# A hybrid S5 and band attention step on one core: band corners written once into the bias table, queries and keys transposed four steps later, third token tile loaded sooner

## The chip, the core and the metric

The kernel runs on one core of one Trainium2 chip. The time is device time in microseconds (us) of one execution, given as the median of several runs. The engines are TensorE (PE; its weight loads are listed apart as PEld), VectorE (DVE), ScalarE (ACT), GpSimd (POOL) and SyncE (SP), which here issues nearly all the DMAs; POOL issues the rest. Each engine works through its instructions in program order, and so does a DMA queue with its issues.

## The reference, cut to what matters

One layer: RMS norm, one input projection into six groups of 512 columns, an S5 branch, band attention, and an output projection. 2048 prompt tokens (16 tiles of 128) and 8x16 tokens of running streams (tile 16).

```
h = _rms_norm(x, norm_gain)
z = jnp.einsum('bld,de->ble', h, w_in)
u, g_s, q, k, v, g_a = jnp.split(z, SPLITS, axis=-1)
y_s, hr, hi = _s5_branch(u, ...)
q = _rms_norm(heads(q), q_gain); k = _rms_norm(heads(k), k_gain)
y_a = _band_attention(q, k, v, rel_table)      # 8 heads x 64, own chunk of 64 and 8 before
mixed = concat([y_s * silu(g_s), y_a * silu(g_a)])
y = x + einsum('ble,ed->bld', mixed, w_out)
...
dist = arange(CHUNK)[:, None] + PAST_CHUNKS * CHUNK - arange(BAND * CHUNK)[None, :]
bias = rel_table[:, clip(dist, -128, 128) + 128]
s = where(valid, q @ k * HEAD_DIM ** -0.5 + bias, NEG_INF)
```

## The kernel before

**The foreground.** Every projection is made of steps, `mm3` (L189 to L191): three matmuls of 128x128 by 128x512, since each 32-bit operand is split into a high and a low part (high by high, low weight by high, high weight by low). `inproj` has three passes over the 17 token tiles in the order 16, 0, 1, ..., 15; pass 1 makes u and k, pass 2 v and q, pass 3 the two gates, 8 steps for each group: 816 steps. Then `glu` has 136 steps and `outproj` 272. A tile's activations come as `xraw` (L214), are split by ACT into `hhi` (L228) and two steps later by DVE into `hlo` (L231). Weights come in chunks of 128x512 (`load_w`, L139, 256 KB) into 5 raw buffers, and `conv_w` splits a chunk on ACT (`whi`, L155) and DVE (`wlo`, L156); the chunk that takes over the raw buffer is loaded right away at the start, and two steps later (`T_LW`) elsewhere. The last tile of a pass converts the 16 chunks of the next pass while it still works with its own.

**Queries and keys** (`ev_norm`). After the eighth step of a group ACT squares and scales the result (L274, L275). Two steps later `power` reduces on DVE (L279) and POOL takes the power (L280, L281); `T_SCALE` = 8 steps after the evacuation `scale` multiplies on DVE (`zs`, L284), and `T_TURN` = 14 steps after it `turn` puts four transposes on PE (L294), whose result ACT and DVE split (L303, L304) and SP stores into `kt_d` or `qt_d` (L244) two steps later and more. These delays are counted in steps by `defer` and `tick`.

**The background** is one generator, `bias_rows`, then `s5`, `decode` and `attention`, that is advanced between steps by a credit: 0.48 of a step's 650 in S5, nothing while weights are being converted, and in attention as many as the work that is left asks for, so that it ends 64 steps before the last. A `yield` of n costs n credits. What it emits stands in the engines' programs between the steps. In S5 of interest: `UT` transposes (P on ACT L719, PE L733, ACT L734) and `build_c` with the matmuls `pk` (L686), which follows the first `feed`.

**The bias.** `bias_rows` writes for each head a skewed table of 128 rows of 767 entries into `tl_d` (L965, one POOL DMA each). In attention each of 32 units loads a 128x640 tile from it (`bias`, L1114, on SP), and POOL sets two 64x64 corners of the tile, which lie outside the band, to a large number (L1115, L1116).

**The start.** `inproj` loads the first two tiles in quarters with 5 weight chunks between, converts chunks 0 to 15, and each conversion issues the load five chunks on; then `dma_h(2)` loads the third tile, and the first 32 steps run.

```
        for j in range(2):
            sumsq(TILES[j], tok[j])
            for _ in range(4):
                self.conv_w()
        dma_h(2)
```

Of the kernel before, what the change touches and what calls it, by code (L numbers as in the profile page):

```python
# [7 lines left out]
F32 = mybir.dt.float32  # L8
# [15 lines left out]
NH, HD = 8, 64  # L24
# [4 lines left out]
BIG = 1e30  # L29


def fv(ap):
    return ap.bitcast(F32)
# [6 lines left out]
def ap_of(t, offset, pat):  # L40
    return bass.AP(tensor=t.tensor, offset=t.offset + offset, ap=pat)


class Build:
# [97 lines left out]
    def conv_w(self):  # L142
        nc = self.nc
        n = self.nconv
        self.nconv += 1
        key, _, k = self.chunks[n]
        raw = self.raws.pop(n)
        hi = self.wp.tile([128, 512], F32R, tag="whi", name="whi", bufs=16)
        lo = self.wp.tile([128, 512], F32R, tag="wlo", name="wlo", bufs=16)
        if k is None:  # L150
            nc.scalar.activation(out=hi, in_=raw, func=AF.Copy)
            nc.vector.tensor_sub(lo, raw, fv(hi))
        else:
            gcol = self.gain[:, k:k + 1]
            nc.scalar.activation(out=hi, in_=raw, func=AF.Copy, scale=gcol)  # L155
            nc.vector.scalar_tensor_tensor(lo, raw, gcol, fv(hi), op0=OP.mult, op1=OP.subtract)  # L156
        self.W[key] = (hi, lo)
        if self.step:
            self.defer(self.T_LW, lambda: self.load_w(n + self.NR))
        else:  # L160
            self.load_w(n + self.NR)

    def due(self, start, gap, n):
        self.cq += [start + gap * j for j in range(n)]
# [28 lines left out]
    def inproj(self):  # L193
        nc, I, tc = self.nc, self.I, self.tc
# [9 lines left out]
        def load_tok(t):  # L204
            xt = xp.tile([128, 1024], F32, tag="xtok", name="xtok")
            nc.sync.dma_start(xt, x3[t])
            return xt

        def dma_h(i):
            if i >= len(seq):  # L210
                return
            ps, t = seq[i]
            raw = hp.tile([128, 8, 128], F32, tag="xraw", name="xraw", bufs=1)
            nc.sync.dma_start(raw, I["xT"][t])  # L214
            XR[i] = raw, load_tok(t) if ps == 0 else None
# [132 lines left out]
        n = 0  # L348
# [17 lines left out]
        for j in range(2):  # L366
            sumsq(TILES[j], tok[j])
            for _ in range(4):
                self.conv_w()
        dma_h(2)  # L370
        for k in range(8):
            for j in range(2):
                self.mm3(z0[j], H0[j][0][:, k], H0[j][1][:, k], W[0, 0, k], k == 0, k == 7)
# [75 lines left out]
    def s5(self):  # L449
        nc, I, tc = self.nc, self.I, self.tc  # L450
# [59 lines left out]
        c = 1.0 / (2.0 * math.pi)  # L510
# [171 lines left out]
        def build_c(b):  # L682

            pk = ps.tile([128, 128], F32, tag="ut", name="pk")
            for g in range(GB):
                nc.tensor.matmul(pk[32 * g:32 * g + 16], X[:, b * GB + g, :],  # L686
                                 CA[b][:, g, 0:8].rearrange("p j h -> p (j h)"), start=True, stop=True,
                                 tile_position=(0, 32 * g))
            KR[b] = pk

        def build_d(b):
            pk = KR[b]
            kr = KR[b] = mp.tile([16, GB, 128], F32, tag="bt", name="kr", bufs=1)
            for g in range(GB):
                nc.scalar.activation(out=kr[:, g], in_=pk[32 * g:32 * g + 16], func=AF.Copy)
            nc.vector.tensor_tensor(out=kr[:, :, 0:16], in0=kr[:, :, 0:16], in1=Deye[:, b * GB:(b + 1) * GB], op=OP.add)

        def build_e(b):
            kr = KR.pop(b)
            for j in range(8):  # L700
                nc.sync.dma_start(Tm[b % 2][16 * j:16 * j + 16, :, 16 * j:128], kr[:, :, 0:128 - 16 * j])  # L701
# [34 lines left out]
        def feed(n):  # L736

            def blk(m):
                return m // 3, m % 3
            if n + 3 < 3 * NBATCH:  # L740
                load_u(*blk(n + 3))
            if n + 1 < 3 * NBATCH:
                perm_u(*blk(n + 1))
            if n < 3 * NBATCH:
                step_a(*blk(n))
# [118 lines left out]
        SL = self.SL_S5  # L864
# [9 lines left out]
        for n in range(3):  # L874
            if n == 1:
                build_d(0)
            feed(n)
            if n == 0:
                build_c(0)
            if n == 2:  # L880
                build_e(0)
            yield SL
# [64 lines left out]
    def bias_line(self):  # L947
        nc, I = self.nc, self.I
        self.st_line = ExitStack()
        c = self.pool(self.st_line, "line", side="right")  # L950
        self.rl = c.tile([NH, 768], F32, name="rl")
        self.rr = c.tile([NH, 257], F32, name="rr")
        nc.gpsimd.dma_start(self.rr, I["rel"])

    def bias_rows(self):

        nc, rl, rr = self.nc, self.rl, self.rr
        nc.vector.tensor_scalar(self.qg2, self.qg2, -0.125, None, op0=OP.mult)
        nc.vector.tensor_scalar(rl[:, 511:768], rr, -1.0, None, op0=OP.mult)
        nc.vector.tensor_scalar(rl[:, 0:511], rr[:, 0:1].to_broadcast([NH, 511]), -1.0, None, op0=OP.mult)  # L960
        nc.gpsimd.dma_start(self.rl_d, rl)
        self.st_line.close()
        yield 600
        for h in range(NH):
            nc.gpsimd.dma_start(self.tl_d[h], ap_of(self.rl_d, 768 * h, [[0, 128], [1, 767]]))  # L965
            yield 1000


    def decode(self):
# [129 lines left out]
    def attention(self):  # L1099
        nc = self.nc  # L1100
        st = ExitStack()
        p = self.pool(st, "att", side="right", bufs=2)
# [8 lines left out]
        def bias(n):  # L1111
            if n < len(heads):
                b = p.tile([128, 640], F32, tag="bias", name="bias", bufs=3)
                nc.sync.dma_start(b, ap_of(self.tl_d, heads[n] * 128 * 767 + 127, [[766, 128], [1, 640]]))  # L1114
                nc.gpsimd.memset(b[64:128, 0:64], BIG)  # L1115
                nc.gpsimd.memset(b[0:64, 576:640], BIG)  # L1116
                BI[n] = b

        def load_k(n, old):
# [139 lines left out]
        SL = self.SL_ATT  # L1259
# [11 lines left out]
        for n in range(2):  # L1271
            bias(n)
            yield 3 * SL
# [4 lines left out]
        for i in range(N + 6):  # L1278
# [9 lines left out]
            if done:  # L1288
                n, s, a = subs[i - 2]
# [28 lines left out]
            if i < N:  # L1318
                n, r = x[0], i % 8
                if r == 2:  # L1320
                    load_ga(n)
                if n + 1 < len(units) and r < 6:
                    loads(n + 1)[r]()
                if r == 3:
                    bias(2 * n + 2)
                if r == 5:
                    bias(2 * n + 3)
# [153 lines left out]
    MARGIN = 0  # L1481
    att_left = 136
    C_PREP = 400
    T_SCALE, T_TURN = 8, 14
    WARM = 24
    A_START = 2
    W_PV, W_QT = 0.3, 1.2
# [119 lines left out]
```

## Time and profile before

| | |
|---|---|
| median of 3 runs | 1228.44 us (1226.21 to 1231.3) |
| the profiled execution | 1226.13 us |
| its span | 1224.3 us, 18936 instructions |
| mean granted TensorE clock | 0.995 of full speed |
| PE, PEld busy | 1193.0 us (97%), 983.1 us (80%) |
| DVE, ACT, POOL busy | 742.6 us (61%), 597.7 us (49%), 366.6 us (30%) |
| mm3 of the input passes (L189, L190, L191) | 339.2, 321.3 and 320.7 us, 816 each |
| DMA | 236.58 MB in 190119 packets, 58136 of them under 512 B |

The span is what the hardware profiler saw of one execution; the 1.8 us between it and the execution's time lie before and after. Busy times are the sums of one engine's instructions. In the timeline a matmul's row has its start and its modelled length, and overlaps the next one: the time that one takes is the distance from start to start, and the square bracket gives the idle time before it with what ended it.

### The profile page before, as it was taken

How to read it: one execution, taken by the hardware profiler on the slowest of the kernel's cores; microseconds unless marked ns; L12 is line 12 of the kernel's file. 1: busy time of each engine (PE TensorE's matmuls, PEld its weight loads, DVE VectorE, ACT ScalarE, POOL GpSimd, SP SyncE). 2: the span in 40 equal slices, each digit the busy share in tenths (PEclk: the TensorE clock that was granted, in tenths of full speed). 3: DMA queues.
4: the chain of work that ended last, by engine and by line, in shares of the span. 5: the costliest groups of instructions: out<-in, count | busy, mean ns of one | idle time of the engine just before them, and what ended most of it. 6: DMA issues, size and time to landing. Idle time of an engine off the chain costs nothing.

```text
span 1224.3 us, 18936 instructions
## 1 busy us (share of the span) xinstructions
PE 1193.0 (97%) x6687; PEld 983.1 (80%) x6687; DVE 742.6 (61%) x1391; ACT 597.7 (49%) x1159; POOL 366.6 (30%) x455
## 2 busy tenths in 40 slices
PE   8999999899999998999999999999999999999998
PEld 5788888777788876887777878788888888888876
DVE  5324556868999988985444456565565555555511
ACT  6434446266666656553232346565654555455410
POOL 2433242557767735540000011111211121121120
PEclk9999999999999998999999999999999999999999
DMA  8876556655545567433895688897877777767243
GB/s 252 262 250 181 155 177 202 195 142 129 149 123 151 135 195 214 110 93 88 270 382 171 204 247 245 255 265 205 217 221 215 206 240 241 196 205 225 73 136 107
DMA packets 190119, 236.58 MB, mean 193 GB/s; under 512 B 58136, under 2 KB 122656, under 8 KB 189000
## 3 DMA queue, kind: packets, MB, share of 16 engines
q1 hardware_dynamic: 189016, 232.15, 64.2%
q0 software_dynamic: 864, 3.21, 0.8%
q8 instruction: 53, 0.87, 0.3%
q14 instruction: 42, 0.34, 0.1%
q10 hardware_dynamic: 144, 0.00, 0.0%
HBM read 169.48 MB, written 67.80 MB: 194 GB/s over the span
## 4 chain that ended last, share of the span: by engine, by line
PE 78%; DMA 6%; DVE 6%; POOL 3%; ACT 3%; issue 2%; SPq 1%; DVEq 0%; ACTq 0%; POOLq 0%
PE z L189 19%; PE z L191 18%; PE z L190 18%; PE o L1218 6%; PE pt L1200 5%; PE s L1170 5%; DMA wraw<-in_w_in_dram 3%; PE pt L294 1%; PE o L1057 1%; PE y L843 1%; SPq L701 1%; PE y L842 1%; PE v L771 1%; ACT whi L155 1%; PE s L1015 1%
## 5 line engine op out<-in xcount | busy, mean ns | idle before, releaser
L189 PE MATMUL z<-whi,hhi 128*128 128x512 f32 x816 | 339.2, 416 | 1.4 <-ACT whi L155 0.7
L190 PE MATMUL z<-wlo,hhi 128*128 128x512 f32 x816 | 321.3, 394 | 3.3 <-DVE wlo L156 3.1
L191 PE MATMUL z<-whi,hlo 128*128 128x512 f32 x816 | 320.7, 393 | 0.5 <-DVE hlo L231 0.5
L189 PEld LDWEIGHTS z<-whi,hhi 128*128 128x128 f32 x816 | 154.1, 189 | 38.9 <-issue 5.1
L190 PEld LDWEIGHTS z<-wlo,hhi 128*128 128x128 f32 x816 | 154.5, 189 | 36.5 <-DVE wlo L156 8.0
L191 PEld LDWEIGHTS z<-whi,hlo 128*128 128x128 f32 x816 | 154.0, 189 | 34.3 <-DVE hlo L231 1.0
L1207 ACT ACTIVATE pth<-pt 128x640 fp32r<-128x640 f32 (+4 forms) x128 | 81.7, 639 | 129.3 <-PE pt L1200 89.4
L1208 DVE TENSOR_TENSOR ptl<-pt,pth 128x640 fp32r<-128x640 f32 (+4 forms) x128 | 94.6, 739 | 60.6 <-ACT pth L1207 59.7
L189 PE MATMUL z<-whi,mh 128*128 128x512 f32 x272 | 113.7, 418 | 0.0
L1115 POOL MEMSET bias<- 64x64 f32 x32 | 4.7, 146 | 363.5 <-DMA bias<-tl_d 250.0
L1189 ACT ACTIVATE sn<-sn,mn 128x640 f32<-128x640 f32 (+4 forms) x128 | 96.9, 757 | 29.5 <-DVE mn L1180 29.4
L191 PE MATMUL z<-whi,ml 128*128 128x512 f32 x272 | 107.1, 394 | 1.3 <-POOL ml L1415 1.3
L190 PE MATMUL z<-wlo,mh 128*128 128x512 f32 x272 | 106.7, 392 | 0.0
L1180 DVE CUSTOM_DVE_ANT_0 sn<-s,bias 128x640 f32<-128x640 f32 (+4 forms) x128 | 93.3, 729 | 11.4 <-PE s L1170 10.4
L1170 PE MATMUL s<-ks,q 128*128 128x320 f32 (+1 forms) x448 | 87.4, 311 | 0.0
L1200 PE MATMUL pt<-ident,sn 128*128 128x128 f32 x560 | 83.0, 274 | 3.9 <-DVE ptl L1208 3.1
L1170 PEld LDWEIGHTS s<-ks,q 128*128 128x128 f32 x448 | 74.7, 188 | 11.1 <-DVE mn L1180 1.2
L1200 PEld LDWEIGHTS pt<-ident,sn 128*128 128x128 f32 x560 | 64.9, 140 | 22.5 <-ACT sn L1189 10.0
L231 DVE TENSOR_TENSOR hlo<-xraw,hhi 128x1024 fp32r<-128x1024 f32 x49 | 60.9, 1242 | 20.7 <-ACT hhi L228 20.6
L280 POOL TENSOR_SCALAR s<-s 128x8 f32<-128x8 f32 x34 | 15.9, 468 | 182.9 <-DVE s L279 182.3
L1228 DVE TENSOR_TENSOR ot<-o,tmp 64x512 f32<-64x512 f32 x32 | 22.0, 689 | 74.5 <-ACT tmp L1226 74.5
L191 PEld LDWEIGHTS z<-whi,ml 128*128 128x128 f32 x272 | 51.0, 188 | 13.2 <-POOL ml L1415 1.7
(268 smaller groups left out, 2171.3 us busy)
## 6 DMA issues: line engine op xcount, KB each, us to landing
xraw<-in_xT_dram SPq DMA_DIRECT2D x49, 512.0 KB, 4.5
q<-qt_d SPq DMA_DIRECT2D x64, 256.0 KB, 8.6
ks<-kt_d SPq DMA_DIRECT2D x28, 512.0 KB, 5.6
vhl<-vp_d SPq DMA_DIRECT2D x28, 512.0 KB, 6.7
wraw<-in_w_in_dram SPq DMA_DIRECT2D x48, 256.0 KB, 4.5
bias<-tl_d SPq DMA_DIRECT2D x32, 320.0 KB, 6.3
mt<-mt_d SPq DMA_DIRECT2D x17, 512.0 KB, 7.4
x<-in_x_dram SPq DMA_DIRECT2D x34, 256.0 KB, 5.8
```

Source lines behind the costliest of these rows:

```text
L189: mm(z, a, whi, start=first, stop=False)
L190: mm(z, a, wlo, start=False, stop=False)
L191: mm(z, b, whi, start=False, stop=last)
L231: nc.vector.tensor_sub(lo, raw, fv(hi))
L1170: nc.tensor.matmul(ps_s[:, bank, 0:wp], Q[n, x2][:, s, 128 * a:128 * a + 128], KS[n][:, s, c0:c0 + wp], start=(x2 == 0), stop=(x2 == 1))
L1180: nc.vector.tensor_tensor_reduce(out=o, in0=i0, in1=i1, scale=1.0, scalar=3e38, op0=OP.add, op1=OP.min, accum_out=mn)
L1189: nc.scalar.activation(out=sn[:, 0:w], in_=sn[:, 0:w], func=AF.Exp, scale=-1.0, bias=mn, accum_out=SUM[n][:, a, s:s + 1])
L1200: nc.tensor.transpose(t[:, k], pr[:, 128 * k:128 * k + 128], self.ident)
L1207: nc.scalar.activation(out=h, in_=t[:, 0:w], func=AF.Copy)
L1208: post.append(lambda: nc.vector.tensor_tensor(out=l, in0=t[:, 0:w], in1=fv(h), op=OP.subtract))
L1218: nc.tensor.matmul(o[:, a0:a1], VB[n][:, j, s, :], t[:, 3 * a0 + j + a0:4 * (a1 - 1) + j + 1:4], start=(y == 0 and j == 4), stop=(y == 1 a ...
L1228: post.append(lambda: nc.vector.tensor_tensor(out=ot[mine], in0=o[mine], in1=tmp[mine], op=OP.add))
```

## The change

1. The corners go into the table: `bias_rows` fills a 64x64 tile `big` once (DVE memset) and, after the eight table writes, issues two POOL DMAs for each head that write it over the two corners of that head's table (16 DMAs of 64 rows of 256 bytes), 500 credits a head. The 64 POOL memsets in attention go.
2. `T_SCALE` is 10 and `T_TURN` 18.
3. The third tile's load, `dma_h(2)`, is issued after the first half of the last eight conversions. The loads of chunks 16 to 20, which the conversions of the start issued, are deferred to steps 40, 50, 60, 70 and 80.
4. A `yield SL` (800 credits) comes between the first `feed` of S5 and `build_c`.

```diff
@@ conv_w
         if self.step:
             self.defer(self.T_LW, lambda: self.load_w(n + self.NR))
+        elif n + self.NR < 16:
+            self.load_w(n + self.NR)
         else:
-            self.load_w(n + self.NR)
+
+            self.defer(40 + 10 * (n + self.NR - 16), lambda: self.load_w(n + self.NR))
@@ inproj
             sumsq(TILES[j], tok[j])
             for _ in range(4):
                 self.conv_w()
-        dma_h(2)
+            if j == 0:
+                dma_h(2)
@@ s5
             feed(n)
             if n == 0:
+                yield SL
                 build_c(0)
@@ bias_line
+        self.big = c.tile([64, 64], F32, name="big")
         nc.gpsimd.dma_start(self.rr, I["rel"])
@@ bias_rows
         nc.gpsimd.dma_start(self.rl_d, rl)
-        self.st_line.close()
+        big = self.big
+        nc.vector.memset(big, BIG)
         yield 600
         for h in range(NH):
             nc.gpsimd.dma_start(self.tl_d[h], ap_of(self.rl_d, 768 * h, [[0, 128], [1, 767]]))
             yield 1000
+
+        for h in range(NH):
+            for p, c in ((64, 0), (0, 576)):
+                nc.gpsimd.dma_start(ap_of(self.tl_d, h * 128 * 767 + 127 + 766 * p + c, [[766, 64], [1, 64]]), big)
+            yield 500
+        self.st_line.close()
@@ attention, bias
                 nc.sync.dma_start(b, ap_of(self.tl_d, heads[n] * 128 * 767 + 127, [[766, 128], [1, 640]]))
-                nc.gpsimd.memset(b[64:128, 0:64], BIG)
-                nc.gpsimd.memset(b[0:64, 576:640], BIG)
                 BI[n] = b
@@
-    T_SCALE, T_TURN = 8, 14
+    T_SCALE, T_TURN = 10, 18
```

Lines of the changed kernel lie 3 to 11 lower: L192 to L194 for the three matmuls, L297 for the transposes, L287 for `zs`, L723, L737 and L738 for P and the `ut` transposes, L690 for `pk`, L775 for `v`.

**SP at the start**, before: the last four weight loads (`wraw`), of which wraw_295 is the last, stand ahead of the third tile.

```order
L139 DMA wraw_277<-in_w_in_dram 128x512
L139 DMA wraw_283<-in_w_in_dram 128x512
L139 DMA wraw_289<-in_w_in_dram 128x512
L139 DMA wraw_295<-in_w_in_dram 128x512
L214 DMA xraw_297<-in_xT_dram 128x1024
```

And now, where wraw_262 is chunk 15 and wraw_473 chunk 16:

```order
L139 DMA wraw_256<-in_w_in_dram 128x512
L139 DMA wraw_262<-in_w_in_dram 128x512
L217 DMA xraw_268<-in_xT_dram 128x1024
L209 DMA xtok_270<-in_x_dram 128x1024
L247 DMA u_d_68<-plain_340 128x512
L247 DMA u_d_68<-plain_342 128x512
L217 DMA xraw_402<-in_xT_dram 128x1024
```

The third tile's load now stands right behind chunk 15; five loads that stood ahead of it are gone from there.

**PE at the end of pass 1**, the last steps of tile 15 (`whi_1956`, `whi_1965` and `whi_1972` are the last three chunks of the new weights), before:

```order
L191 MATMUL z_1989<-whi_1956,hlo_1779 128x512
L294 MATMUL pt_2028<-ident_82,zs_1905 128x128 x4
L189 MATMUL z_1989<-whi_1965,hhi_1778 128x512
L190 MATMUL z_1989<-wlo_1966,hhi_1778 128x512
L191 MATMUL z_1989<-whi_1965,hlo_1779 128x512
L189 MATMUL z_1989<-whi_1972,hhi_1778 128x512
```

And now, the names of the last two chunks being whi_1964 and whi_1972:

```order
L194 MATMUL z_1986<-whi_1964,hlo_1772 128x512
L192 MATMUL z_1986<-whi_1972,hhi_1771 128x512
L193 MATMUL z_1986<-wlo_1973,hhi_1771 128x512
L194 MATMUL z_1986<-whi_1972,hlo_1772 128x512
L192 MATMUL z_2037<-whi_1793,hhi_1915 128x512
L193 MATMUL z_2037<-wlo_1794,hhi_1915 128x512
L194 MATMUL z_2037<-whi_1793,hlo_1916 128x512
L192 MATMUL z_2037<-whi_1804,hhi_1915 128x512
L193 MATMUL z_2037<-wlo_1805,hhi_1915 128x512
L194 MATMUL z_2037<-whi_1804,hlo_1916 128x512
L297 MATMUL pt_2049<-ident_82,zs_1898 128x128 x4
```

The transposes have moved behind both of those weight steps and behind two steps of the next group, whose weights were made long before.

**PE at the end of pass 2.** Before, the same four transposes (and eight small S5 matmuls) stood ahead of the last two weight steps. Now S5's `ut` transposes (L737) of P_4751 stand there, ahead of chunk 14 (`whi_4717`) and chunk 15 (`whi_4725`):

```order
L194 MATMUL z_4742<-whi_4708,hlo_4525 128x512
L737 MATMUL ut_4800<-ident_82,P_4751 128x16 x4
L192 MATMUL z_4742<-whi_4717,hhi_4524 128x512
L193 MATMUL z_4742<-wlo_4718,hhi_4524 128x512
L194 MATMUL z_4742<-whi_4717,hlo_4525 128x512
L192 MATMUL z_4742<-whi_4725,hhi_4524 128x512
```

and on ACT, which makes P_4751, now:

```order
L155 ACTIVATE whi_4717<-wraw_4682,gain_86 128x512
L155 ACTIVATE whi_4725<-wraw_4694,gain_86 128x512
L326 ACTIVATE th_4737<-z_4657,hrstd_93 128x512
L723 ACTIVATE P_4751<-U_4141 16x512
L738 ACTIVATE UT_4439<-ut_4753 128x4x128
```

P stands behind the split of chunk 15 and behind a gate's `th`, while the transposes that read it stand ahead of the steps with chunks 14 and 15.

## Rows read from the trace of the kernel before

**Rows 1.** Page, busy time (us, share of the span, count) and the chain that ended last.

```profile
PE 1193.0 (97%) x6687; PEld 983.1 (80%) x6687; DVE 742.6 (61%) x1391; ACT 597.7 (49%) x1159; POOL 366.6 (30%) x455
...
PE 78%; DMA 6%; DVE 6%; POOL 3%; ACT 3%; issue 2%; SPq 1%; DVEq 0%; ACTq 0%; POOLq 0%
```

**Rows 2.** Waits of PE: us in total, times, longest us.

```profile
PE pt L294 <- DVE zs L284: 6.4, 5, 2.4
...
PE pk L686 <- ACT UT L734: 2.0, 1, 2.0
...
PE tm L1359 <- POOL ms L1400: 1.2, 1, 1.2
```

**Rows 3.** Busy us by stretch: length, PE, PEld, DVE, ACT, POOL; then clock, DMA share, GB/s.

```profile
210.00:240.00 30.00, 27.58 (x118) 22.12 (x117) 27.63 (x52) 11.78 (x17) 14.16 (x13) 0.94 0.69 208
240.00:270.00 30.00, 27.02 (x137) 21.46 (x135) 17.66 (x30) 15.67 (x33) 16.95 (x21) 1.00 0.48 131
450.00:480.00 30.00, 25.68 (x121) 19.16 (x121) 24.63 (x36) 17.66 (x34) 13.54 (x14) 0.89 0.83 256
475.00:478.00 3.00, 3.00 (x8) 2.32 (x9) 2.86 (x6) 1.20 (x5) 1.45 (x3) 0.50 1.02 318
690.00:720.00 30.00, 28.54 (x141) 23.15 (x140) 15.86 (x33) 13.49 (x28) 1.86 (x5) 1.00 0.80 247
690.00:900.00 210.00, 203.28 (x1168) 172.72 (x1167) 126.03 (x266) 121.13 (x261) 36.35 (x56) 1.00 0.80 234
900.00:1140.00 240.00, 240.00 (x1412) 209.98 (x1410) 134.79 (x263) 122.58 (x227) 39.31 (x53) 1.00 0.74 216
```

**Rows 4.** Chain of waits, 20 to 36 us: start us, us, what.

```profile
22.50 4.11 DMA wraw<-in_w_in_dram
...
28.55 4.71 DMA xraw<-in_xT_dram
```

**Rows 5.** Timeline of PE, 32 to 37 us: start us, us, what [idle before <-releaser].

```profile
34.80 0.39 PE L190 MATMUL z<-wlo,hhi 128*128 128x512 f32 x1
35.72 0.50 PE L191 MATMUL z<-whi,hlo 128*128 128x512 f32 x1 [0.53 <-DVE hlo L231]
...
36.30 0.40 PE L190 MATMUL z<-wlo,hhi 128*128 128x512 f32 x1
36.53 0.40 PE L191 MATMUL z<-whi,hlo 128*128 128x512 f32 x1
```

**Rows 6.** Timeline of all engines, end of pass 1.

```profile
217.23 0.75 DVE L156 SCALAR_TENSOR_TENSOR wlo<-wraw,gain,whi 128x512 fp32r<-128x512 f32 x1 [0.80 <-ACT whi L155]
217.90 0.68 DVE L284 TENSOR_TENSOR zs<-zs,s 128x512 f32<-128x512 f32 x1
...
218.73 0.69 PE L294 MATMUL pt<-ident,zs 128*128 128x128 f32 x4 [2.17 <-DVE zs L284]
```

**Rows 7.** Timeline of all engines, end of pass 2.

```profile
469.74 0.73 ACT L155 ACTIVATE whi<-wraw,gain 128x512 fp32r<-128x512 f32 x1 [1.88 <-DMA wraw<-in_w_in_dram]
...
469.76 0.50 PE L190 MATMUL z<-wlo,hhi 128*128 128x512 f32 x1 [0.83 <-DVE wlo L156]
...
470.38 0.67 ACT L323 ACTIVATE th<-z,hrstd 128x512 f32<-128x512 f32 x1
...
472.84 1.09 PE L294 MATMUL pt<-ident,zs 128*128 128x128 f32 x4 [2.35 <-DVE zs L284]
```

**Rows 8.** Groups of line L719: duration ns min/median/max, first and last start us, forms.

```profile
L719 ACT ACTIVATE P<-U x24: 610/626/647, 245.6 to 523.8; 128x512 f32<-128x512 f32 x16, 16x512 f32<-16x512 f32 x8
```

**Rows 9.** Tile tl_d: duration ns min/median/max of the issues, and its landings.

```profile
L965 POOL DMA_DIRECT2D tl_d<-rl_d x8: 523/626/662, 37.6 to 73.6; - x8
...
DMA to landing us min/median/max: 4.9/6.7/9.8
```

**Rows 10.** Timeline of POOL, 80 to 100 us.

```profile
83.04 0.20 POOL L280 TENSOR_SCALAR s<-s 128x8 f32<-128x8 f32 x1 [7.57 <-DVE s L279]
```

**Rows 11.** Waits of POOL: us in total, times, longest us.

```profile
POOL bias L1115 <- DMA bias<-tl_d: 250.0, 30, 16.1
```

## The prediction

> **What bounds the kernel.** I read the page's busy times and chain first. PE is busy 97% of the span and holds 78% of the chain [rows 1], so time can come only out of PE's idle stretches and out of stretches at a lower clock; 1224.3 - 1193.0 = 31 us are idle. The change removes no matmul. Second come the waits of PE, to see which of the idle time the changed lines own [rows 2]: the transposes of queries and keys waited 6.4 us in five places for `zs`, the S5 matmul `pk` 2.0 us, a transpose of the S5 output 1.2 us for a POOL product. Third come the windows, for the clock [rows 3]: 30 us around the end of pass 1 have a mean granted clock of 0.94 and those around the end of pass 2 one of 0.89, and 475 to 478 us stand at 0.50, which is the 1.2 GHz level; the other stretches of that group have 1.00. The timelines then show what came before: an idle of 2.17 us at 218.7 [rows 6] and one of 2.35 us at 472.8 [rows 7], both ended by `zs`. The 2.0 us before `pk` [rows 2] lie in 240 to 270 us, whose clock is 1.00 [rows 3]. Fourth, the attention stretch: 900 to 1140 us has 240.00 of 240 us busy, 690 to 900 us 203.28 of 210 [rows 3]; there only small gaps are to be had.
>
> **Third tile.** The chain of the start is xraw's issue at 28.55, landing 4.71 us later, its split on ACT, and `hlo` on DVE [rows 4]; PE waits for that and goes from 34.80 to 35.72 for what takes 0.23 a little later, from 36.30 to 36.53 [rows 5], so 0.7 us are lost. Chunk 15's own landing begins at 22.50 [rows 4], and xraw now stands right behind that load on SP. An issue at about 23 lands at about 28 even at 4.71 us, 5 us sooner, against an idle of 0.53 [rows 5], so `hlo` is ready before it is needed. **-0.7 us**, bounds 0 and -0.9. The five deferred weight loads (5 x 256 KB = 1.3 MB, 6 us at the 216 GB/s that 900 to 1140 us moves without any PE gap [rows 3]) come one every ten steps; chunk 16 is converted only at step 260, 220 steps after its load. I cost them at nothing; if one delays a tile, its price is of the size of rows 5's 0.7.
>
> **End of pass 1.** Lost before: 2.17 us of idle, and a clock of 0.94 over 30 us is 3.6 us at half speed, of which half, 1.8, is lost; together 4.0. On DVE `zs` stood behind the `wlo` of chunk 15 (217.23 + 0.75, then 0.68 [rows 6]). Now the steps with chunks 14 and 15 come first, then two steps with old weights, then the transposes. PE, free at 218.73 - 2.17 = 216.56, is through with chunk 14 at 217.25 at 3 x 0.23 a step, and finds the `wlo` of chunk 15 at 217.98: 0.7 of wait. After that it has 1.4 us of work, while DVE owes `zs` and one or two other pieces of 0.7: at most 0.7 again. Two waits of 0.7 are each shorter than the 2.0 that left the clock alone. 4.0 - 1.4 = **-2.6 us**, bounds 0 (late weights) and -4.0.
>
> **End of pass 2.** Lost before: 0.83 for a weight and 2.35 for `zs` [rows 7], and 0.89 over 30 us is 6.6 us at half speed; taking off the idle at its front I put 2.7 on it: 5.9. Here I don't expect the same gain, because the order of the change puts the `ut` transposes ahead of chunk 14's step, and ACT makes their P behind the split of chunk 15, behind `th`. In times of before: split at 469.74, 0.73 long, `th` 0.67 [rows 7], P 0.63 [rows 8], so P at 471.8. PE, without its 0.83, is done with chunk 13 at about 469.5. It idles 2.3 us, more than 2.17, so the clock should drop again. 2.3 + 2.7 = 5.0 remain: **-0.9 us**, bounds 0 and -5.9. Those 2.3 us shift with weights and PE alike; under 2.0 the clock would probably hold.
>
> **Other waits.** Three more waits of transposes hold 6.4 - 2.17 - 2.35 = 1.9 us; with `zs` issued two steps later and read six, now eight, steps after it, all go: **-1.9**. The `yield` ahead of `build_c` is 800 credits at 0.48 x 650 = 312 a step, 2.6 steps or, at 3 x 0.23 = 0.69 a step [rows 5], 1.8 us of other matmuls, so of 2.0 at `pk` about 0.3 stays: **-1.7**. Attention loses 64 memsets and with them POOL's stand behind each bias load. Of those waits, 250 us in 30 places [rows 11], all but one are off PE's path; the one that isn't delays a product at 771 us, 1.2 us [rows 2]: **-1.2**.
>
> **What is added.** The corner writes cost 4000 credits, 12.8 steps, with the `yield` 15.4 steps or 10.6 us at 0.69: S5 stands that much later against the foreground, and so its transposes meet other tile ends. Such a meeting costs between nothing and the 2.35 us of rows 7 with a clock drop behind it, 5 us; `pk` with its 2.0 [rows 2] is such a meeting, and I take half of that once more, **+1.0**. The 16 issues by POOL cost 0.63 each at most [rows 9], 10 us in three tiles, and POOL is idle 7.6 us before the power of each tile [rows 10]: nothing, as long as an issue doesn't wait for a landing. The landing of a table write took 4.9 to 9.8 us [rows 9], so the other bound is 16 x 6.7 = 107 us less 3 x 7.6 = 23, or +84; the order of the program makes a corner write wait only for the DMA eight places before it, so I take nothing and keep +84 as a rival. Against this change speaks the Trainium skill, DMA: Bandwidth & Descriptors, section on the anatomy of one gpsimd DMA: a DMA costs about 2.0 us plus its bytes at 436 GB/s. By that the 16 writes of 16 KB, if POOL stood through each, would be an estimated 33 us, 10 more than its idle time, and the sum 1230. For a table write of 393 KB the same formula gives 2.9 us, and this trace has 4.9 to 9.8 to landing but 0.63 on POOL, so the measured rows decide: the engine is free long before.
>
> **Sum.** -0.7 - 2.6 - 0.9 - 1.9 - 1.7 - 1.2 + 1.0 = -8.0 against the profiled execution's 1226.13: 1218.1. The median of the runs is 1228.44, 2.3 above it, so 1220.4, or **1220** as a median.
>
> **Rivals.**
> - Pass 2 keeps its clock: P comes under 2.0 us late, since the stores of kt and qt no longer stand between the last weight loads. 2.7 less, and the +1.0 is not needed: 1216.5. For it: 2.3 lies near the border. Against it: P is behind chunk 15 on the same engine whatever the loads do.
> - The waits change owner: the last weight chunks arrive as late as before, PE idles over 2.17 us for them and the clock drops at both ends. The 2.6 and 0.9 go, and new S5 stalls cost another 1.0: 1225. For it: the 0.83 for a weight stands right ahead of the 2.35 for `zs` [rows 7]; against it: only 0.7 stays at pass 1 by rows 6.
> - Slower: attention begins 10.6 us later and must end at the same step, so its share of each step grows by 10.6/470, 2%. If that is the point where DVE, ACT and the loads no longer keep ahead of PE, every 30 us from 690 to 1140 loses what 690:720 loses, 1.46 [rows 3]: 15 x 1.46 = 21.9, less the 210 - 203.28 = 6.7 already lost there, +15.2: 1235. For it: 690 to 900 already shows such gaps, at a DMA share of 0.80. Against it: 900 to 1140 has none, with DVE at 56% and ACT at 51%.
> - POOL stands in the corner writes: late powers, late `zs`, late transposes from 80 us on; between +10 and +84, 1230 to 1304. It decides if an issue waits for the landing of the one ahead.
>
> **How the numbers follow.** Under 0.5%, 6.1 us, a measurement of this kernel can't tell a difference from none: the borders are 1222.3 and 1234.6. The forecast has 0.45 (its own range 1216 to 1224; 0.36 of it below 1222.3), the kept clock 0.20, the changed owner 0.22, squeezed attention 0.09, POOL 0.04. Faster: 0.36 + 0.20 = 0.56. Same: 0.09 + 0.20 of the changed owner + 0.04 of attention + 0.02 of POOL = 0.35. Slower: 0.02 + 0.05 + 0.02 = 0.09. The range takes in the kept clock with a bound beyond it (pass 2 saving up to 5.9), 1212, and the changed owner with another lost clock, 1229; it leaves out the squeezed attention and POOL, and a little at each end.
>
> **What would show it.** Right: xraw issued near 23 us and no gap at 35; no wait of the transposes for `zs` over 0.7; a clock of 1.00 from 210 to 240; `pk` waiting under 0.5; no POOL wait for a bias load and none of a PE transpose for POOL near 771; 900 to 1140 still full. At the end of pass 2 the wait of `ut` for P near 2.3 and a window at 0.50 behind it. Wrong: the clock low after 218 us, waits of L193 for `wlo` over 1 us at both ends of passes, gaps after 900 us, or transposes waiting for POOL's power from 80 us on.

## The result and the profile after

The changed kernel takes 1240.03 us (median, 1239.23 to 1242.66) against 1228.65 us for the kernel before in the same comparison: ratio 1.0096, interval 1.0070 to 1.0122. It is slower by 11 us, where 8 us faster were forecast. The profiled execution has a span of 1238.0 us. Its page, busy time and chain, beside [rows 1]:

```profile
PE 1197.8 (97%) x6687; PEld 984.5 (80%) x6687; DVE 735.1 (59%) x1392; ACT 596.6 (48%) x1159; POOL 359.9 (29%) x407
...
PE 70%; DVE 10%; DMA 9%; ACT 4%; SPq 3%; issue 3%; POOL 1%; DVEq 0%; ACTq 0%
```

PE has the same 6687 instructions. Its share of the chain fell from 78% to 70%, and DVE and DMA took over: PE waits more often. The waits of PE, beside [rows 2]:

```profile
PE z L193 <- DVE wlo L156: 5.7, 12, 1.5
PE ty L1355 <- DMA y<-y_d: 5.0, 1, 5.0
...
PE z L192 <- DVE vhl L255: 3.7, 1, 3.7
PE v L775 <- DVE t L795: 3.4, 3, 1.8
PE ut L737 <- ACT VB L683: 2.7, 2, 1.5
```

All three waits of [rows 2] are gone, the transposes' 6.4 us for `zs`, 2.0 at `pk` and 1.2 for POOL. In their place stand others that the kernel before had smaller or not at all. The stretches of [rows 3], with one more (720 to 750 us, whose clock was 1.00 before):

```profile
210.00:240.00 30.00, 27.93 (x123) 21.44 (x122) 27.74 (x63) 13.74 (x20) 10.33 (x9) 1.00 0.67 208
240.00:270.00 30.00, 26.23 (x125) 20.50 (x124) 14.74 (x22) 13.06 (x25) 20.88 (x26) 0.94 0.54 151
450.00:480.00 30.00, 27.55 (x125) 21.06 (x124) 23.39 (x36) 18.74 (x33) 13.62 (x15) 0.94 0.84 254
...
720.00:750.00 30.00, 26.62 (x136) 22.04 (x137) 12.35 (x34) 14.27 (x35) 3.85 (x3) 0.89 0.89 265
690.00:900.00 210.00, 201.18 (x1126) 170.02 (x1124) 118.53 (x252) 114.87 (x248) 29.23 (x23) 0.98 0.79 230
900.00:1140.00 240.00, 236.16 (x1390) 205.94 (x1391) 133.80 (x262) 122.57 (x228) 34.59 (x19) 1.00 0.76 224
```

The low clock of 210 to 240 us is gone, that of 450 to 480 is half gone, and it is new at 240 to 270 and 720 to 750; 900 to 1140, full before, has lost 3.8 us. In SyncE's timeline the third tile's load now starts 5.6 us sooner than in [rows 4]:

```profile
21.22 1.65 SPq L139 DMA_DIRECT2D wraw<-in_w_in_dram  x3
22.92 0.42 SPq L217 DMA_DIRECT2D xraw<-in_xT_dram  x1
```

To see where the time goes, the two traces are set side by side by the foreground's steps, each at the start of its third matmul. Up to step 288 nothing of S5 is on PE, and at step 816 all of S5 and decode is done, so differences between these points are time lost or gained. To step 256 the change gains 1.9 us (0.4 of them four transposes that now come behind that step), to step 288 (just past the end of pass 1 at 272) another 1.0; from there to step 816 it loses 8.7, and from 816 to the end 8.3 (together 14.1, against 13.7 between the two spans). Of the 8.7, 5.4 are more idle of PE (15.6 us against 10.2), 0.4 those transposes, and 2.9 PE's other work taking longer, with 6.8 us at half clock in both kernels; where those 2.9 come from was not traced.

Two places stand out in PE's timeline.

```profile
245.78 0.59 PE L192 MATMUL z<-whi,hhi 128*128 128x512 f32 x1 [3.66 <-DVE vhl L255]
246.16 0.63 PE L193 MATMUL z<-wlo,hhi 128*128 128x512 f32 x1
...
723.26 0.72 PE L1355 MATMUL ty<-ident,y 128*128 128x128 f32 x4 [5.01 <-DMA y<-y_d]
723.77 0.76 PE L192 MATMUL z<-whi,yh 128*128 128x512 f32 x1
724.33 0.63 PE L193 MATMUL z<-wlo,yh 128*128 128x512 f32 x1
```

Both idles are followed by matmuls of 0.63 instead of 0.39 us, starting 0.43 apart instead of 0.23: half clock. At the first, DVE works on S5's set-up (`build_a` and what precedes it) without a break, and `vhl`, which frees PE's next accumulator, stands behind it:

```profile
241.81 1.11 DVE L672 TENSOR_TENSOR VBp<-X,ArD 128x512 f32<-128x512 f32 x1
242.83 1.21 DVE L673 TENSOR_TENSOR btmp<-Xs,AiS 128x512 f32<-128x512 f32 x1
244.07 0.99 DVE L674 TENSOR_TENSOR VBp<-VBp,btmp 128x512 f32<-128x512 f32 x1
244.99 0.74 DVE L255 SCALAR_TENSOR_TENSOR vhl<-z,rstd,vhl 128x512 fp32r<-128x512 f32 x1
```

At the second, SyncE's timeline shows attention's first loads (`q`) behind the weights of glu and outproj and ahead of the `y` tile that glu waits for. That load takes 8.55 us in the chain, where the one that was waited for before took 5.26. In the kernel before the same `q` loads went out at 681 to 687 us, ahead of those weights. First the change:

```profile
708.76 1.57 SPq L139 DMA_DIRECT2D wraw<-in_w_out_dram  x3
710.38 1.14 SPq L1145 DMA_DIRECT2D q<-qt_d  x2
...
712.19 1.49 SPq L1145 DMA_DIRECT2D q<-qt_d  x2
714.57 0.33 SPq L1347 DMA_DIRECT2D y<-y_d  x1
...
714.57 8.55 DMA y<-y_d
```

and the kernel before:

```profile
681.44 1.24 SPq L1134 DMA_DIRECT2D q<-qt_d  x2
...
702.53 5.26 DMA y<-y_d
```

S5's first transposes start at 258.7 us (248.0 before), attention's first products at 730.8 (709.7). Counted in foreground steps both come 13 steps later (335 against 322, 833 against 820). The forecast shift is there, with a price that was not forecast.

### The profile page after: what moved, and what is told of

Read it like the earlier page. It is cut to its first block, busy times and chain, and to the rows that moved or that the text cites. A ratio compares the mean times of both kernels' runs of the same rounds, so it can differ in the third digit from the quotient of the medians.

```text
span 1238.0 us, 18836 instructions
## 1 busy us (share of the span) xinstructions
PE 1197.8 (97%) x6687; PEld 984.5 (80%) x6687; DVE 735.1 (59%) x1392; ACT 596.6 (48%) x1159; POOL 359.9 (29%) x407
## 4 chain that ended last, share of the span: by engine, by line
PE 70%; DVE 10%; DMA 9%; ACT 4%; SPq 3%; issue 3%; POOL 1%; DVEq 0%; ACTq 0%
PE z L192 16%; PE z L194 16%; PE z L193 16%; PE o L1229 5%; PE pt L1211 5%; PE s L1181 5%; DMA wraw<-in_w_in_dram 3%; SPq L705 1%; DMA mt<-mt_d 1%; DVE hlo L234 1%; PE o L1070 1%; PE pt L297 1%; DVE wlo L156 1%; DMA T<-kr 1%; PE v L775 1%
## 5 line engine op out<-in xcount | busy, mean ns | idle before, releaser
L192 PE MATMUL z<-whi,hhi 128*128 128x512 f32 x816 | 339.8, 416 | 4.7 <-DVE vhl L255 3.7
L194 PE MATMUL z<-whi,hlo 128*128 128x512 f32 x816 | 320.5, 393 | 0.0
L192 PEld LDWEIGHTS z<-whi,hhi 128*128 128x128 f32 x816 | 154.1, 189 | 42.8 <-issue 4.8
L194 PEld LDWEIGHTS z<-whi,hlo 128*128 128x128 f32 x816 | 153.8, 188 | 33.3
L192 PE MATMUL z<-whi,mh 128*128 128x512 f32 x272 | 114.2, 420 | 0.0
L194 PE MATMUL z<-whi,ml 128*128 128x512 f32 x272 | 107.1, 394 | 0.4 <-POOL ml L1426 0.4
L1411 POOL TENSOR_TENSOR ms<-ms,gs 128x512 f32<-128x512 f32 x16 | 20.6, 1288 | 240.9 <-DMA gs<-gs_d 116.4
L1426 POOL TENSOR_TENSOR ml<-mt,mh 128x1024 fp32r<-128x1024 f32 x17 | 40.7, 2394 | 163.3 <-ACT mh L1425 148.5
L282 DVE TENSOR_REDUCE s<-sq 128x8 f32<-128x512 f32 x34 | 23.1, 680 | 80.4 <-ACT sq L277 80.4
L283 POOL TENSOR_SCALAR s<-s 128x8 f32<-128x8 f32 x34 | 15.6, 458 | 176.9 <-DVE s L282 176.4
```

The lines of the kernel that those rows point to most:

```text
L192: mm(z, a, whi, start=first, stop=False)
L194: mm(z, b, whi, start=False, stop=last)
L1426: self.defer(2, lambda: self.nc.gpsimd.tensor_tensor(out=lo, in0=m, in1=fv(hi), op=OP.subtract))
```

## The experiments

Theory A: the 4800 credits that the change adds (4000 with the corners, 800 with the `yield`) move S5, decode and attention against the foreground, and that costs all the loss. Rival B: the later scaling and transposing. Rival C: the corner writes. Rival D came up for the gap before 723 us: that the other parts are needed for it. Each kernel ran 4 to 10 times; ratios are against the kernel before in the same comparison (medians 1225.8 to 1227.3 us). Statements by step or by wait are from one profiled execution of each kernel.

| kernel | median us | ratio, interval |
|---|---|---|
| the change, 4000 credits taken back | 1230.65 | 1.0032, 1.0011 to 1.0053 |
| before + 4000 credits | 1236.49 | 1.0091, 1.0062 to 1.0120 |
| before + later scale and turn | 1227.45 | 1.0012, 0.9992 to 1.0032 |
| the change, old scale and turn | 1234.70 | 1.0073, 1.0055 to 1.0091 |
| before + 4000 credits + yield | 1244.39 | 1.0122, 1.0082 to 1.0162 |
| the change without the yield | 1232.10 | 1.0044, 1.0028 to 1.0059 |
| before + start alone | 1223.23 | 0.9966, 0.9951 to 0.9982 |
| before + start + corners, no credits | 1223.68 | 0.9975, 0.9956 to 0.9993 |
| before + yield alone | 1229.96 | 1.0022, 1.0004 to 1.0039 |
| before - 4000 credits | 1234.07 | 1.0064, 1.0040 to 1.0087 |
| before + 2000 credits | 1237.08 | 1.0090, 1.0060 to 1.0120 |
| start + corners + later turn, no credits | 1221.92 | 0.9967, 0.9955 to 0.9979 |
| before, decode and attention later | 1237.01 | 1.0087, 1.0058 to 1.0116 |
| the change, all 4800 credits back | 1229.94 | 1.0030, 1.0019 to 1.0041 |

**The delay taken out of the change, and put alone into the kernel before.**

```diff
@@ bias_rows of the change, behind each table write
-            yield 1000
+            yield 500
@@ bias_rows of the kernel before, behind each table write
-            yield 1000
+            yield 1500
```

> The change with 500 instead of 1000 credits behind each of the eight table writes, so that the table and corner writes together cost the 8000 credits that the table alone cost before; everything else of the change stays. Theory A (the 4000 added credits put S5, decode and attention some 9 to 11 us later against the foreground, and the new stalls come from that): S5's first ut transposes come back from 258.7 to about 248 to 250 us, the 5.2 us gap of the glu transposes before 723 us and the 3.8 us gap at 246 us go, and the time is 1218 to 1228 us. Rival B (the later scaling and transposing of queries and keys causes the stalls): the time stays at 1237 to 1243 us wherever S5 stands. Rival C (the corner writes themselves, by POOL or by what reads the table): also 1237 to 1243 us.

> The kernel before with 1500 instead of 1000 credits behind each of the eight table writes: the 4000 added credits alone, no corner writes by DMA, the old delays for queries and keys, the old start. Theory A: slower than before by 8 to 17 us, 1236 to 1245 us, with a gap of the glu transposes of several us near 715 to 725 us. Rivals B and C: within 3 us of before, 1226 to 1232 us.

Measured: 1230.65, and 1236.49 for the delay alone, 10.7 above the kernel before with nothing else changed. The gap before 723 us is gone in the first (its longest wait of a transpose for `y` is 1.29 us, 1.35 before). In the second it isn't there either (0.24 us), although theory A expected it. The delay alone makes the kernel slow, so neither B nor C is needed for most of the loss. But the first misses its range by 2.7 us at the upper end: something besides the 4000 credits costs.

**The transposes alone, and taken out of the change.**

```diff
-    T_SCALE, T_TURN = 8, 14
+    T_SCALE, T_TURN = 10, 18
```

> The kernel before with T_SCALE, T_TURN of 10, 18 alone. Theory A: faster by 3 to 7 us, 1221 to 1226 us, the waits of the transposes for zs (6.4 us) gone and no low clock after 219 us. Rival B: slower than before, 1232 us or more. Rival C: as theory A.

> The change with T_SCALE, T_TURN back at 8, 14; corners, third tile, deferred loads, the added credits and the yield stay. Theory A: no better than the change, 1240 to 1247 us. Rival B: 1224 to 1230 us. Rival C: 1240 to 1247 us.

Measured: 1227.45, no difference from before, and 1234.70, a ratio of 1.0073 beside the change's 1.0096: without the later turn the loss is still there, so B falls as its cause. Theory A missed both: 3 to 7 us were expected to be saved in the first, and 1240 us or more in the second. The waits of PE in the run with the later turn alone, and two stretches of it, show why:

```profile
PE z L190 <- DVE wlo L156: 5.1, 10, 1.5
...
PE z L189 <- DVE vhl L252: 2.2, 2, 1.2
...
PE z L189 <- ACT zs L275: 1.6, 2, 1.4
```

```profile
210.00:240.00 30.00, 26.24 (x113) 19.67 (x112) 27.48 (x51) 13.78 (x21) 11.15 (x11) 1.00 0.72 213
450.00:480.00 30.00, 24.83 (x131) 18.87 (x130) 24.06 (x35) 15.96 (x30) 11.97 (x11) 1.00 0.76 234
```

The 6.4 us for `zs` are gone and the clock holds at 1.00 in these two stretches, yet by steps the kernel is level with the kernel before (-0.3 us at step 288, counting in the four transposes that are still to come, and +1.4 at 576). Waits for `wlo`, for `vhl` and for an accumulator have come instead, and a new stretch at half clock at 250.8 us. DVE has 27.48 us of work in the 30 us at the end of pass 1, as before (27.63). With the engine that is waited for this full, moving one reader of it moved the wait to the next reader.

**The two delays of the change together, and the change with 4000 of them.**

```diff
@@ bias_rows and s5 of the kernel before
-            yield 1000
+            yield 1500
...
+                yield SL
                 build_c(0)
@@ s5 of the change
-                yield SL
                 build_c(0)
```

> The kernel before with 1500 credits behind each table write and the yield of 800 ahead of the first pk matmuls: the whole 4800 credits of the change without any other part of it. Theory A, in its strict form (the place of S5 and attention sets the time): 1236 to 1242 us, with a gap of 3 us or more of the glu transposes waiting for their y load, as in the change and as with the old delays for queries and keys, and not in the run with 4000 alone. Rival D (the early third tile and the removed memsets are needed for that gap): 1232 to 1238 us and no such gap.

> The change without the yield ahead of the first pk matmuls: 4000 credits of delay are left. Theory A: still slower than before by 5 to 14 us, 1231 to 1240 us; if the gap before 723 us depends on the last 800 credits, it is gone and the time is 1231 to 1235. Rival D: the gap stays, 1237 to 1242.

Measured: 1244.39 and 1232.10. The 4800 credits alone cost 18 us in the medians (10 to 20 by the ratio's interval), no less than the whole change, and bring the gap for `y` with them (3.30 us of idle); in the change with 4000 of them the longest wait for `y` is 1.26. Rival D falls: the gap needs the later attention and no other part. It comes in all four kernels whose first attention product stands at step 833 (3.3 to 5.0 us), and in neither of the two with 4000 credits, where it stands at 831. What the other parts give back is not sharper than that interval.

**The parts that save.** The start alone is part 3 of the change in the kernel before; the second kernel is the change with part 3 and with the corners, whose credits are taken from the tables.

```diff
@@ the second, against the change
-            yield 1000
+            yield 500
...
-                yield SL
                 build_c(0)
...
-    T_SCALE, T_TURN = 10, 18
+    T_SCALE, T_TURN = 8, 14
```

> The kernel before with the third tile's load issued after the first half of the conversions and the loads of chunks 16 to 20 deferred, nothing else. All theories: the 0.7 us gap at 35.7 is gone and 1.2 to 2 us are saved by step 32 to 48; Theory A: these stay saved to the end, 1223 to 1226 against 1225.8 of before. Rival D: the earlier foreground moves S5 against it and gives back some of it, 1226 to 1231.

> Corner writes without added credits (500 behind each table write and 500 behind each head's corners) with the third tile and the deferred loads; the old delays for queries and keys and no yield. Theory A: faster than before by 2 to 5 us, 1221 to 1224, since nothing is shifted, the start saves 1.2 to 2 and no product in attention waits behind a bias load (1.2). Rival C (the corner writes by themselves cost): slower than the run with the start alone by 3 us or more.

Measured: 1223.23 and 1223.68. The start saves 2.8 us. The corners without credits change nothing that can be told from it, so C falls. In the profiled execution of the second, PE waited 2.77 us at 54.4 us: four table writes went out in 2.2 us, SyncE's store `ksd` of that moment held its buffer until ACT had waited 11.47 us for it, and the next tile's result came late. By step 64 this cost 4.6 us in that execution. The first corner write went out only at 59.4 us, so it is not theirs.

**How the place counts.** The yield alone, the kernel before with 4000 credits fewer and with 2000 more, and all but the yield without added credits.

```diff
@@ s5 of the kernel before, the yield alone
             if n == 0:
+                yield SL
                 build_c(0)
@@ bias_rows of the kernel before, 4000 fewer
-            yield 1000
+            yield 500
@@ bias_rows of the kernel before, 2000 more
-            yield 1000
+            yield 1250
@@ the change, without credits and yield
-            yield 1000
+            yield 500
...
-                yield SL
                 build_c(0)
```

> The kernel before with the yield of 800 credits ahead of the first pk matmuls alone. Theory A: the 2.2 us before pk shrink to below 1, but all of S5 behind it, decode and attention stand 1.8 us later; by the jump between 4000 credits (plus 10.7) and 4800 (plus 18) such a shift can cost: 1225 to 1230 us. Theory A2 (any shift costs about in proportion, 10.7 for 4000): plus 2 less 1.5, 1226 to 1228.

> The kernel before with 500 instead of 1000 credits behind each table write: S5, decode and attention stand 4000 credits or 9 us sooner. Theory A2 (lateness costs: the longer attention has, the better): faster, 1216 to 1222 us. Theory A3 (the kernel before stands at a good place by its tuning, and any shift meets other tile ends): slower, 1230 to 1238 us.

> The kernel before with 1250 credits behind each table write, 2000 in all or 4.4 us of delay. Theory A2: 1230 to 1233 us. Theory A3: anything from 1226 to 1240, not between the times of 0 and 4000 credits by need.

> Corners without added credits, the third tile and the deferred loads, and T_SCALE, T_TURN of 10, 18; no yield. It stands beside the run with the old delays for queries and keys (1223.7) and the one with the yield too (1230.7). Theory A with the result of the turn alone (plus 1.6): 1223 to 1226, so that the yield is what costs 5 us. Rival B: 1228 to 1231, so that the later transposes cost them.

Measured: 1229.96, 1234.07, 1237.08 and 1221.92. Against the credits the kernel before goes 1234.1 (-4000), 1226 (0), 1230.0 (the yield's 800), 1237.1 (+2000), 1236.5 (+4000), 1244.4 (+4800): it is worse on both sides, and 2000 cost as much as 4000. So it is neither lateness nor a price by the credit (A2 falls) but the place. Of the losses with -4000, +2000 and +4000, 4.1, 3.5 and 3.7 us lie ahead of step 256 in the profiled executions, where the third tile landed late with no S5 on PE yet; that part is not S5's place, and why it came in just these was not tried. Some 4, 7.5 and 7 us are left, still worse on both sides. The last of the four has every part of the change but the added credits and the yield, and it beats both kernels: this pair (1221.92 against 1240.03) shows the shift as the cause of the loss.

**Which pieces.** Decode and attention alone later, S5 where it was; and the whole change with 500 behind the tables and 400 behind the corners, so that everything behind the yield stands in its old place.

```diff
@@ background of the kernel before
             yield None
+        yield 7500
         yield from self.decode()
@@ bias_rows of the change, behind each table write and behind each head's corners
-            yield 1000
+            yield 500
...
-            yield 500
+            yield 400
```

> The kernel before with 7500 credits between S5 and decode: S5 stands where it stood, decode and attention come some 15 steps or 10 us later, as in the change. If the late start of attention (its first loads beside the glu weights and the y loads) is what costs, 1236 to 1244 us, with the gap of the glu transposes near 720 us; if S5's place against the foreground costs, 1225 to 1231 us.

> All parts of the change, the yield of 800 too, with 500 credits behind each table write and 400 behind each head's corners, so that everything behind the yield stands where it stood before and only S5's first pieces come 800 credits sooner. Theory A3 (the place counts): 1219 to 1225 us, as without the yield (1221.9). If the yield costs by what it separates and not by the shift: 1228 to 1232, as with it and 800 credits more (1230.7).

Measured: 1237.01 and 1229.94. The second misses theory A3's range and lies in that of the yield's own price; what it lost is read below. The first loses 13.4 us behind step 816 and nothing ahead of it. Its PE timeline has the change's gap, and its windows the change's loss in attention:

```profile
715.77 0.72 PE L1344 MATMUL ty<-ident,y 128*128 128x128 f32 x4 [4.81 <-DMA y<-y_d]
```

```profile
900.00:1140.00 240.00, 236.29 (x1391) 206.06 (x1390) 133.91 (x261) 123.42 (x228) 39.24 (x53) 1.00 0.74 217
```

Waits of 0.57 us for `sn` that the change has at 1013.6 us come here at 1010.8: in both the same transposes of attention stand at step 1035. That second half of the change's loss is the later attention. For the first half, from step 288 to 816, no run puts S5 alone in the change's place, so it is argued from the traces: the wait for `vhl` behind S5's batch (3.7 us), S5's own waits for DVE and ACT at `v` and `ut` (3.4 and 2.7 us, 0.2 and 1.3 before), less the 6.2 us for `zs` and at `pk` that went there. The last kernel shows in one place what a shift can do. By steps it is within 1.1 us of the best kernel (1221.92) up to step 288 and behind step 816; between those it loses 9.9 against it. Of these 5.5 are one wait, some 1.8 the half clock behind it (0.94 in the 30 us on either side of 240), and 2.0 longer waits for `vhl`. The timeline of all engines in the change with all credits back:

```profile
237.62 0.99 DVE L674 TENSOR_TENSOR VBp<-VBp,btmp 128x512 f32<-128x512 f32 x1
238.53 1.21 DVE L287 TENSOR_TENSOR zs<-zs,s 128x512 f32<-128x512 f32 x1
...
239.80 1.12 PE L297 MATMUL pt<-ident,zs 128*128 128x128 f32 x4 [5.50 <-DVE zs L287]
```

and DVE's in the best kernel (1221.92), which has no yield, where the same `zs` comes ahead of the batch:

```profile
232.61 0.68 DVE L287 TENSOR_TENSOR zs<-zs,s 128x512 f32<-128x512 f32 x1
...
234.46 0.76 DVE L663 TENSOR_TENSOR CA<-PB,ArS 128x576 f32<-128x576 f32 x1
...
239.18 1.00 DVE L674 TENSOR_TENSOR VBp<-VBp,btmp 128x512 f32<-128x512 f32 x1
```

To keep its successors in place the background had to start 800 credits sooner, and six DVE instructions of `build_a`, some 6 us, slipped ahead of one `zs`. Here 1.8 us of a piece's place are worth 5.5 us of idle and a stretch at half clock behind it. So the yield doesn't cost by what it separates: the change with 4000 credits taken back has it too, with S5's first pieces in their old place, and is level with the best kernel at step 320, where this one is 7.8 us behind.

## Why the prediction was wrong

**What is added** is the step that failed. It gave the shift of S5 +1.0, by half of one wait at `pk`, and the rest of the sum stood on the waits that go. The credits alone measured +10.7 (4000, of which 3.7 lie ahead of step 256 and are not S5's place) and +18.3 (4800). The size of the shift was forecast right, 10.6 us against 10.7 at S5's first transposes; what it meets was not worked out, though the order of the program shows which DVE rows stand ahead of which. The term stood for one meeting of 2 us; the runs show several, with half clock behind some of them. A background that is placed by hand against tile ends had no price per microsecond here: each of its pieces has to be examined at its new place, S5's batch on DVE above all, and its first loads against what else SyncE issues there. Two of the signs that the prediction named for being wrong came: waits for `wlo` over 1 us at both ends of passes, and gaps after 900 us.

**Third tile**: right, and under-sized (0.7 was forecast, 0.9 at most). The gap at 35 us is gone; 1.6 us are saved by step 256, in the change (1.9 less the 0.4 of later transposes) as in the kernel with the start alone, and there 2.8 us to the end in the medians. The deferred loads cost nothing.

**End of pass 1**: -2.6 was forecast, -1.0 came. The clock held and no transpose waits. But the step with the new weights waits 1.50 us for `wlo`, not 0.7:

```profile
217.11 0.50 PE L193 MATMUL z<-wlo,hhi 128*128 128x512 f32 x1 [1.50 <-DVE wlo L156]
...
220.58 0.60 PE L297 MATMUL pt<-ident,zs 128*128 128x128 f32 x4
```

PE comes to the weights sooner once the transposes are out of its way, and DVE, busy for 27.74 of these 30 us, is no faster. That the clock held is partly luck: in two of the six kernels with the later turn (1221.92 and 1232.10) it stood at 0.50 from 217 or 218 us all the same. With the old delays it fell there in all ten.

**End of pass 2**: the forecast wait of `ut` for P didn't come. ACT had no weight load to wait for (1.88 us in [rows 7]) and was through with the split of chunk 15 at 467.90 us, 2.6 sooner than before, so P was ready at 468.98; and PE, itself held by `wlo`, came to `ut` only at 470.09:

```profile
465.35 2.55 ACT L155 ACTIVATE whi<-wraw,gain 128x512 fp32r<-128x512 f32 x4
...
468.37 0.61 ACT L723 ACTIVATE P<-U 16x512 f32<-16x512 f32 x1
...
469.43 0.50 PE L193 MATMUL z<-wlo,hhi 128*128 128x512 f32 x1 [1.49 <-DVE wlo L156]
...
470.09 0.42 PE L737 MATMUL ut<-ident,P 16*128 16x16 f32 x4
...
472.43 0.63 PE L192 MATMUL z<-whi,hhi 128*128 128x512 f32 x1
```

The clock fell all the same, but for 3.4 us and not 6.8. Idle and half clock together cost some 7.2 us before and 5.4 now between steps 528 and 576 (an estimate from 4.3 and 3.7 us of idle, and half of 5.7 and of 3.4 us of work at half clock): more than the forecast 0.9 was saved, by another way than the one that was forecast.

**Other waits**: the five of the transposes, the one at `pk` and the one for POOL at 771 us went, as forecast; the time didn't. The first was moved to other readers of DVE, shown by the later turn alone (no difference). The second was bought with the shift: the yield alone costs 0.22% (0.04 to 0.39). Of the third nothing could be told from zero.

**Corner writes**: POOL stood 0.52 to 0.63 us in each and they landed in 3.2 to 5.5 us; its wait for the reductions of the norms is much as before (176.4 us in 28 places, 182.3 in as many before). Taking the measured rows over the formula of the Trainium skill, DMA: Bandwidth & Descriptors, section on the anatomy of one gpsimd DMA (an estimated 2.04 us for each of 16 KB), was right for POOL; to landing they took longer than it gives.

**Rivals**: the squeezed attention, given 0.09, named the right side and half of the mechanism: attention later, 900 to 1140 us no longer full. It was priced by 30 us windows and by density; what came is one load of `y` behind attention's own first loads (5.0 us and half clock) and 3.8 us of small waits. Pass 2 with its clock kept (0.20) had its condition, P in time, but not its result. The changed owner (0.22) named the weights as the next thing that PE waits for, which came, with 1.5 us at each end. No rival had S5's set-up in front of `vhl` or `zs`.

## What to carry to other kernels

Where a second stream of work is laid between the steps of a first by a count, an edit that adds to the count moves all that follows: give the credit back in the same edit, or price the move by itself before the parts. A saved wait is worth something only if the engine that was waited for has time to spare there; here, at 27 busy us out of 30, the wait went to the next reader. The parts without the shift are worth 0.33% (1221.92 us), which can't be told from the start alone (0.34%), and the shift cost 1.3% (a ratio of 1.0096 against 0.9967).

## What the runs showed of the hardware

The length of an idle alone didn't tell whether the granted clock falls, as the forecast had taken it from two idles of 2.17 and 2.35 us and one of 2.0. The wait of 2.0 to 2.1 us at `pk`, behind 5 us at full clock, occurs in six kernels; the clock stayed at 1.00 behind it in four and stood at 0.50 within 1.6 us of its end in two. Here are two of equal length, in the kernel with the later turn alone, where the clock fell,

```profile
250.50 0.44 PE L686 MATMUL pk<-CA,X 128*16 128x128 f32 x8 [2.11 <-ACT UT L734]
...
251.46 0.63 PE L190 MATMUL z<-wlo,hhi 128*128 128x512 f32 x1
```

and in the best kernel, where it didn't:

```profile
249.22 0.41 PE L690 MATMUL pk<-CA,X 128*16 128x128 f32 x8 [2.11 <-ACT UT L738]
...
250.37 0.40 PE L192 MATMUL z<-whi,hhi 128*128 128x512 f32 x1
```

In the change the clock stood at 0.50 from 471.5 to 474.5 us behind an idle of 1.49 us and two of 0.3 ahead of it; in the change without the yield (1232.10) 2.72 us of idle up to 475.8 were followed by full clock:

```profile
475.00:480.00 5.00, 4.22 (x26) 3.71 (x27) 4.86 (x12) 2.63 (x5) 3.42 (x5) 1.00 0.48 132
```

A store of SyncE's was slower beside several DMAs of POOL's. The store of 256 KB into `ksd` at some 42 us holds a buffer that ACT writes next. In the five kernels with 500 credits behind the table writes, POOL issues four of these writes (393 KB each) within 3 us of the store, and ACT's next write comes 9.7 to 12.1 us after the store's issue. In the eleven kernels with 1000 credits or more one or two go out so near to it, and ACT's write comes after 5.9 to 8.5. Two of these kernels, the kernel before (6.8) and the one with 4000 credits fewer (9.7), differ in nothing else. The kernel before, and the one with start and corners, whose store went out at 40.38:

```profile
49.87 0.69 ACT L303 ACTIVATE kt<-pt,kg 128x512 fp32r<-128x512 f32 x1 [6.91 <-DMA ksd<-kt]
...
52.49 0.69 ACT L306 ACTIVATE kt<-pt,kg 128x512 fp32r<-128x512 f32 x1 [11.47 <-DMA ksd<-kt]
```
